# The prompt's keys are turned, and its final states taken, one place later, behind the first half of the first gate tile

## The chip, the cores and the metric

The program runs on one core of a Trainium2 chip. The metric is the device time of one execution in microseconds; the kernel before takes 1621.96 us as the median of three runs (1619.52 to 1623.79).

## What is computed

One step of a two-layer diffusion backbone on 512 latent tokens and 128 prompt tokens, width 1024. Layer 0 mixes tokens by pooling, layer 1 by bidirectional retention with 4 heads; a squared-ReLU MLP follows each. The retention of one head, cut to what matters here:

```
q, k, v, g = split(h @ w_in)                      # per head: q, k 256 wide, v, g 512 wide
q, k (latent only) are rotated by grid position
state_dir = sum over prompt tokens  zeta_dir * k^T v        # final prompt states, an output
o = intra(q, k, v) + q @ cached_state (latent only), both directions
out = (silu(g) * groupnorm(o)) @ w_out
returns y_prompt, y_sample, new_state_ret         # new_state_ret: 2 directions x 4 heads x 256 x 512
```

The final prompt states (`new_state_ret`) are read by nothing else in the kernel: they are computed and written out.

## The kernel before

All products are done in a split form: each fp32 operand is cut into a high part (a copy on ScalarE, ACT, line 144) and a low part (a subtraction on VectorE, DVE, line 145), and `mm3` (lines 205 to 207) issues three matmuls: high by high, high by low, low by high. A `gemm` is one output tile of 128 features by 320 tokens (half of the 640): 8 blocks of the contraction times 3 matmuls, 24 in all.

Layer 1 runs a loop over the four heads (`for hd in range(HEADS)`). Ahead of each pass lie the values of the head (`values`, lines 990 to 992 for the products) and its queries and keys (`take`, lines 935 to 948: a copy of two halves, the prompt's part `pr` by line 938, the rotation). For head 0 the order is keys, then values; for heads 1 to 3 it is values, output projection of the head before, queries and keys, and the very last thing ahead of the pass is the second key tile. Then one pass is, in the order of the program:

1. `states`, first part: two transposes of the prompt's keys into one PSUM tile (line 1005), and for each direction a scaled high part on ACT (line 1011) and a low part on DVE (line 1012), called kz below.
2. `attention`, ahead of its products: decay tables xi and dm (lines 1045 to 1050; dm is an Exp on ACT), and the first operands from the cached state: a load of 256 KB on SP's queue (line 1055), its mean (lines 967, 968), its centred high and low part (lines 974, 975), and a decayed query (line 1058).
3. `step1`: one step of the layer's modulation vectors: it turns the sums of the last step (four transposes, line 394, a reduction, line 395) and makes 16 sums on DVE (lines 387, 389).
4. gate tile 0, as two gemms of 24 matmuls, each ended by a Silu on ACT (line 1031). After each half the generator `final` is advanced by one place.
5. (head 0 alone: another `step1`), gate tile 1 in the same way, another `step1`.
6. `attend`: products with the cached state (tiles 0 and 1 of the forward direction), scores of four key tiles, outputs, then the backward direction; its later state operands are loaded and prepared as they are needed.

The second and third place of `states` are the products of one direction each: two PSUM tiles of three matmuls of 512 columns, each copied out by ACT (line 1020) and written to memory by a transfer from GpSimd's queue (line 1021). With one place taken ahead of the gate, the products of the forward direction stand behind the first half of gate tile 0 and those of the backward direction behind its second half.

The program is written in Tile: the instructions are put down in one order, and a planner makes of it, at compile time, a fixed order for each engine and gives out the slots of the pools. The working tiles of this stage (`t5`, `th`) share one pool of 7 slots of 128 by 512; the scaled prompt keys, the high and low part of the prompt's values, the decay pieces, the cached states as loaded, the decayed queries, the score tiles and the states on their way out all take their slots there. PSUM has 8 banks, all in one pool.

Of the kernel before, what the change touches and what calls it, by code (L numbers as in the profile page):

```python
# [110 lines left out]
def hybrid_kernel(ctx: ExitStack, tc: tile.TileContext, x_prompt, x_sample, state_ret, c, c_ctx, w_ada, b_ada,  # L111
# [71 lines left out]
    def weights(src, pools=(wsp,), other=0):  # L183


        k = src.shape[0] // 128
        wide = 1024 // k
        raw, parts = {}, {}

        def get(j):  # L190
            i = j * 128 // wide
            if i not in parts:
                if i // 2 not in raw:
                    raw[i // 2] = load(src[:, i // 2 * 2 * wide:(i // 2 + 1) * 2 * wide], (k, 2 * wide))
                parts[i] = split_w(raw[i // 2][:, :, i % 2 * wide:(i % 2 + 1) * wide], sub=G if i < other else V,
                                   pool=pools[i % len(pools)])
            o = j * 128 % wide
            return [z[:, :, o:o + 128] for z in parts[i]]

        return get  # L200
# [296 lines left out]
    def add_to_x(d, h, ps, gate):  # L497
        for j, cols in PARTS[h]:
            x = xT[d][:, HALVES[h]][:, cols]
            V.scalar_tensor_tensor(x, ps[:, cols], gate[:, d, j:j + 1], x, ALU.mult, ALU.add)  # L500
# [406 lines left out]
    with tc.tile_pool(name="ret", bufs=1) as rp:  # L907
# [70 lines left out]
        def values(hd):  # L978

            out = [bank() for _ in range(5)]  # L980
            c0 = 2048 + hd * DV
            for e in range(2):
                st = load(ret_w_in[0, e * 512:(e + 1) * 512, c0:c0 + 512], (4, 512))
                for f in range(2):
                    w = split_w(st[:, 2 * f:2 * f + 2])
                    for i in range(5):
                        for k in range(2):
                            hh = [z[:, i * 128:i * 128 + 128] for z in h1t[e * 4 + f * 2 + k]]
                            first, last = e == 0 and f == 0 and k == 0, e == 1 and f == 1 and k == 1
                            T.matmul(out[i], hh[0], w[0][:, k, :], start=first, stop=False)  # L990
                            T.matmul(out[i], hh[1], w[0][:, k, :], start=False, stop=False)  # L991
                            T.matmul(out[i], hh[0], w[1][:, k, :], start=False, stop=last)  # L992
            vs = [centre(out[i], *[rp.tile([128, DV], F32R, tag=f"v{i}{e}", name=nm("v")) for e in "hl"])
                  for i in range(4)]
            vpr = t5()
            vpc = rp.tile([128, DV], F32, tag="vpc", name=nm("vpc"))
            S.copy(vpr, out[4])
            V.tensor_scalar(vpc, vpr, mean_of(vpr), None, ALU.add)
            return vs, split(vpr, t5().bitcast(F32R), t5().bitcast(F32R)), vpc

        def states(hd, prm, vpr):

            pk = bank()
            for t in range(2):
                T.transpose(pk[:, t * 128:(t + 1) * 128], prm["k", t], ident)
            kz = []
            for rr in range(2):
                both = t5().bitcast(F32R)
                hi, lo = both[:, 0:256], both[:, 256:512]
                z = zeta[:, 4 * rr + hd:4 * rr + hd + 1]  # L1010
                S.activation(hi, pk[:, 0:256], AF.Copy, scale=z)
                V.scalar_tensor_tensor(lo, pk[:, 0:256], z, hi.bitcast(F32), ALU.mult, ALU.subtract)
                kz.append((hi, lo))
            yield
            for rr in range(2):
                for t in range(2):
                    pst = bank()
                    mm3(pst, [z[:, t * 128:(t + 1) * 128] for z in kz[rr]], vpr, True, True)
                    so = t5()
                    S.copy(so, pst)  # L1020
                    nc.gpsimd.dma_start(out=new_state[0, 0, rr, hd, t * 128:(t + 1) * 128, :], in_=so)
                yield

        def gates(hd):

            get = weights(ret_w_in[0, :, 4096 + hd * DV:4096 + (hd + 1) * DV])

            def one(e, mid=None, between=None):
                sg = rp.tile([128, TOK], F32, tag=f"sg{e}", name=nm("sg"))
                for h in range(2):  # L1030
                    S.activation(sg[:, HALVES[h]], gemm([get(e)], h1t, h, mid if h == 0 else None)[0], AF.Silu)
                    if between:
                        next(between, None)
                return sg
            return one

        def attention(hd, rot, prm, vs, vpc):

            lf, lb, nlb = lg[:, hd:hd + 1], lg[:, 4 + hd:5 + hd], nlg[:, 4 + hd:5 + hd]
            xi = [rp.tile([128, TOK], F32, tag=f"sg{3 - r}", name=nm("xi"))[:, 0:LAT] for r in range(2)]  # L1040
            for r in range(2):
                S.activation(xi[r], ipos[:, r, :], AF.Exp, scale=(lf, lb)[r])

            dm = rp.tile([128, 896], F32, tag="dm", name=nm("dm"))
            V.tensor_scalar(dm, npos, 0.0, lf, ALU.max, ALU.mult)
            for cols in (slice(0, 448), slice(448, 896)):
                t = t5()[:, 0:448]
                V.tensor_scalar(t, npos[:, cols], 0.0, nlb, ALU.min, ALU.mult)
                V.tensor_tensor(dm[:, cols], dm[:, cols], t, ALU.add)
            S.activation(dm, dm, AF.Exp)  # L1050

            def state_operands(r, t):

                st = t5()
                nc.sync.dma_start(out=st, in_=state_ret[0, 0, r, hd, t * 128:(t + 1) * 128, :])
                sh_, sl_ = centre(st, r5(), r5())
                qx = t5()
                V.tensor_tensor(qx, rot["q", t][0], xi[r], ALU.mult)
                return sh_, sl_, split(qx, r5(), r5())

            first = state_operands(0, 0)
            return lambda: attend(hd, rot, prm, vs, vpc, dm, state_operands, first)
# [49 lines left out]
        def gated(hd, gate, sg, osl, po):  # L1112

            sqs = [Squares(ones_v, GN_EPS * DV / 128), Squares(ones_v, GN_EPS * DV / 128)]
            pe = [po[:, e * 128:(e + 1) * 128] for e in range(4)]
            for e in range(4):
                sqs[0].add(osl[e][:, 0:HALF])
                sqs[1].add(osl[e][:, HALF:LAT], pe[e])
            r = []
            sg.append(gate(2, lambda: r.extend([sq.rstd() for sq in sqs])))  # L1120
            us = [slots(2 * e, TOK) for e in range(4)]
            for e in range(4):
                if e == 2:
                    sg.append(gate(3))
                w = vec[:, O_GN + hd * 4 + e:O_GN + hd * 4 + e + 1]
                V.scalar_tensor_tensor(sg[e][:, 0:LAT], osl[e], w, sg[e][:, 0:LAT], ALU.mult, ALU.mult)
                V.scalar_tensor_tensor(sg[e][:, LAT:TOK], pe[e], w, sg[e][:, LAT:TOK], ALU.mult, ALU.mult)
                for h in range(2):
                    u = th()
                    V.tensor_tensor(u, sg[e][:, HALVES[h]], r[h], ALU.mult)  # L1130
                    split(u, *[z[:, HALVES[h]] for z in us[e]])
            return us
# [14 lines left out]
        for hd in range(HEADS):  # L1147
            gate = gates(hd)
            final = states(hd, qk[1], vv[1])
            next(final)  # L1150
            attn = attention(hd, *qk, vv[0], vv[2])
            step1()
            sg = [gate(0, between=final)]
            if hd == 0:
                step1()
            sg.append(gate(1, between=final))
            step1()
            us = gated(hd, gate, sg, *attn())
            step1()
            get = weights(ret_w_out[0, hd * DV:(hd + 1) * DV])  # L1160
            if hd < HEADS - 1:
                vv = values(hd + 1)
                step1()
                for n in range(KD):
                    for h in range(2):
                        add_to_x(n, h, gemm([get(n)], us, h)[0], mod[1][2])
                qk, _, singles = queries_keys(hd + 1)
                for u in singles:
                    u()
            else:  # L1170
                sq = tail(lambda n, h: gemm([get(n)], us, h)[0], mod[1][2], normed(norm2))
# [34 lines left out]
    final = []  # L1206
# [39 lines left out]
```

## Time and profile before

| what | value |
|---|---|
| median of three runs | 1621.96 us |
| lowest, highest | 1619.52, 1623.79 us |
| the profiled execution, its own time | 1622.77 us |
| its span | 1621.0 us |
| granted TensorE clock, mean | 0.994 of full speed |

The span is what the profiler sees between the first and the last instruction; the 1.77 us around it belong to the time as well. PE stands for TensorE, PEld for its weight loads, ACT for ScalarE, DVE for VectorE, SP for SyncE and its DMA queue. PE is busy for 98% of the span, so a microsecond of any other engine counts only if PE waits for it. The four passes of the head loop begin at about 626, 775, 920 and 1073 us of the span.

### The profile page before, as it was taken

To read this page: it belongs to the slowest core of one execution; us is meant where nothing else is said; L and a number is where in the kernel's file an instruction comes from. 1 tells how busy PE (TensorE), PEld (TensorE's weight loads), DVE (VectorE), ACT (ScalarE), POOL (GpSimd) and SP (SyncE) were. 2 spreads that over 40 slices of the span, in tenths; PEclk is the share of its full clock that TensorE was granted. 3 is DMA by queue.
4 is the path that set the end of the run, shared out by engine and by line. 5 is a ranking of instruction groups with operands and counts; after the bars stand their busy time and mean duration, and the time that the engine had idled before them with its cause. 6 is when DMAs were issued, how large, how long until landed. Compare 5 with 4: busy or idle time off the path is not lost. (4 is left out here: it accounts for less than half of the span.)

```text
span 1621.0 us, 24493 instructions
## 1 busy us (share of the span) xinstructions
PE 1582.8 (98%) x9897; PEld 1473.6 (91%) x9897; DVE 1164.0 (72%) x2254; ACT 727.0 (45%) x1338; POOL 11.7 (1%) x26
## 2 busy tenths in 40 slices
PE   6999999999999999999999999999999999999997
PEld 3459999999999988889889988998899999999997
DVE  6879996676766687886797678778967573554654
ACT  6747326336156354433442443353464371451640
POOL 0000000000000000000000000000000000000000
PEclk9999999999999999999999999999999999999999
DMA  9744333333314123323304241322032132131221
GB/s 356 252 141 146 105 105 104 104 124 111 105 53 156 45 70 128 96 79 130 128 29 156 63 146 64 118 92 91 26 105 79 34 124 78 53 104 53 95 75 66
DMA packets 137954, 169.83 MB, mean 105 GB/s; under 512 B 3512, under 2 KB 111472, under 8 KB 137840
## 3 DMA queue, kind: packets, MB, share of 16 engines
q1 hardware_dynamic: 134800, 161.28, 30.2%
q0 software_dynamic: 1312, 4.20, 0.8%
q10 hardware_dynamic: 1728, 2.78, 0.5%
q8 instruction: 78, 1.28, 0.3%
q14 instruction: 36, 0.29, 0.1%
HBM read 161.43 MB, written 6.82 MB: 104 GB/s over the span
## 5 line engine op out<-in xcount | busy, mean ns | idle before, releaser
L144 ACT CAST whi<-wst 128x1024 fp32r<-128x1024 f32 x245 | 254.4, 1049 | 422.5 <-PE ps L206 200.8
L145 DVE TENSOR_TENSOR wlo<-wst,whi 128x1024 fp32r<-128x1024 f32 x245 | 297.3, 1223 | 136.5 <-ACT whi L144 124.0
L205 PE MATMUL ps<-a,whi 128*128 128x320 f32 x896 | 277.2, 310 | 1.2 <-ACT a L144 1.2
L206 PE MATMUL ps<-a,whi 128*128 128x320 f32 x896 | 277.3, 310 | 0.1
L207 PE MATMUL ps<-a,wlo 128*128 128x320 f32 x896 | 276.2, 309 | 0.0
L500 DVE SCALAR_TENSOR_TENSOR xall<-ps,mod,xall 128x320 f32<-128x320 f32 (+2 forms) x288 | 115.7, 436 | 151.6 <-PE ps L207 150.4
L206 PEld LDWEIGHTS ps<-a,whi 128*128 128x128 f32 x896 | 168.2, 188 | 2.1 <-DVE a L145 1.7
L205 PEld LDWEIGHTS ps<-a,whi 128*128 128x128 f32 x896 | 167.9, 188 | 1.8 <-ACT a L144 1.7
L207 PEld LDWEIGHTS ps<-a,wlo 128*128 128x128 f32 x896 | 168.0, 188 | 0.0
L389 DVE SCALAR_TENSOR_TENSOR acc<-wst,c,acc 128x256 f32<-128x256 f32 x336 | 137.6, 483 | 0.0
L205 PE MATMUL ps<-tq,whi 128*128 128x320 f32 x288 | 89.0, 309 | 0.0
L206 PE MATMUL ps<-tq,whi 128*128 128x320 f32 x288 | 89.0, 309 | 0.0
L207 PE MATMUL ps<-tq,wlo 128*128 128x320 f32 x288 | 89.0, 309 | 0.0
L206 PE MATMUL ps<-A,whi 128*128 128x320 f32 x256 | 78.9, 309 | 0.0
L205 PE MATMUL ps<-A,whi 128*128 128x320 f32 x256 | 78.9, 312 | 0.0
L207 PE MATMUL ps<-A,wlo 128*128 128x320 f32 x256 | 78.2, 309 | 0.0
L145 DVE TENSOR_TENSOR a<-t,a 128x320 fp32r<-128x320 f32 x128 | 61.8, 488 | 22.7 <-ACT a L144 22.2
L435 ACT ACTIVATE t<-xall 128x320 f32<-128x320 f32 x56 | 26.0, 471 | 81.2 <-DVE xall L500 81.2
L852 ACT ACTIVATE t<-t 128x320 f32<-128x320 f32 x128 | 60.5, 473 | 1.8
L144 ACT CAST a<-t 128x320 fp32r<-128x320 f32 x128 | 58.5, 457 | 1.5
L207 PEld LDWEIGHTS ps<-tq,wlo 128*128 128x128 f32 x288 | 54.1, 188 | 0.0
L205 PEld LDWEIGHTS ps<-tq,whi 128*128 128x128 f32 x288 | 54.1, 188 | 0.0
(406 smaller groups left out, 4004.4 us busy)
## 6 DMA issues: line engine op xcount, KB each, us to landing
wst<-in_mlp_w_dram SPq DMA_DIRECT2D x64, 1024.0 KB, 5.3
wst<-in_w_ada_dram SPq DMA_DIRECT2D x46, 1024.0 KB, 6.0
wst<-in_ret_w_in_dram SPq DMA_DIRECT2D x24, 1024.0 KB, 5.2
wst<-in_ret_w_out_dram SPq DMA_DIRECT2D x8, 1024.0 KB, 5.0
t<-in_state_ret_dram SPq DMA_DIRECT2D x16, 256.0 KB, 5.5
out_dram<-t POOLq DMA_DIRECT2D x16, 256.0 KB, 2.9
xt<-in_x_sample_dram SPq DMA_DIRECT2D x4, 512.0 KB, 4.8
both<-in_w_ada_dram SPq DMA_DIRECT2D x2, 1024.0 KB, 7.3
```

Of the source, the lines that this page charges most:

```text
L144: S.copy(hi, src)
L145: sub.tensor_tensor(lo, src, hi.bitcast(F32), ALU.subtract)
L205: T.matmul(out, wh, ah, start=first, stop=False, skip_group_check=more)
L206: T.matmul(out, wh, al, start=False, stop=False, skip_group_check=more)
L207: T.matmul(out, wl, ah, start=False, stop=last, skip_group_check=more)
L389: V.scalar_tensor_tensor(acc[j], w[:, k], by, acc[j], ALU.mult, ALU.add)
L435: S.activation(sq[:, o:o + t.shape[-1]], t, AF.Square)
L500: V.scalar_tensor_tensor(x, ps[:, cols], gate[:, d, j:j + 1], x, ALU.mult, ALU.add)
L852: S.activation(f, r, AF.Square)
```

## The change

The first advance of `final` ahead of the pass is left out. Everything that `states` does happens one place later: the two transposes and the scaled keys behind the first half of gate tile 0, the forward direction's products behind its second half, the backward direction's behind the first half of gate tile 1, and the call behind the second half of gate tile 1 finds the generator at its end. No instruction is added or taken away.

```
         for hd in range(HEADS):
             gate = gates(hd)
             final = states(hd, qk[1], vv[1])
-            next(final)
             attn = attention(hd, *qk, vv[0], vv[2])
             step1()
             sg = [gate(0, between=final)]
```

`final` is used by the loop of `one` in `gates` (`if between: next(between, None)` behind each half), which is unchanged.

## Rows read from the trace of the kernel before

**Rows 1.** The page's head and its part 1 (busy us, share of the span, instructions) for TensorE and its weight loads.

```profile
span 1621.0 us, 24493 instructions
...
PE 1582.8 (98%) x9897; PEld 1473.6 (91%) x9897; DVE 1164.0 (72%) x2254; ACT 727.0 (45%) x1338; POOL 11.7 (1%) x26
```

**Rows 2.** Busy time of each engine in a stretch: the whole retention part, 585 to 1180 us (columns: the stretch, its length, busy us and instructions of PE, PEld, DVE, ACT and POOL, granted clock, DMA share, GB/s).

```profile
...
585.00:1180.00 595.00, 586.03 (x3374) 533.98 (x3373) 465.81 (x995) 237.93 (x437) 8.71 (x16) 0.99 0.29 96
```

**Rows 3.** What PE's matmuls waited for, two stretches, 585 to 1180 us first and then heads 1 to 3 (668 to 1100 us) alone: us in total, times, longest us.

```profile
...
PE ps L1005 <- ACT pr L938: 2.8, 5, 1.4
PE ps L205 <- ACT r L144: 2.3, 5, 0.8
...
PE ps L1005 <- ACT pr L938: 0.8, 3, 0.2
```

**Rows 4.** PE in order of time where head 0's values begin (start us, busy us, engine, line, operation, idle before and what ended it), and below it the clock of the stretch behind the gap (TensorE alone).

```profile
...
595.66 0.39 PE L991 MATMUL ps<-whi,h0l 128*128 128x512 f32 x1
597.41 0.33 PE L1005 MATMUL ps<-tab_sb,pr 128*128 128x128 f32 x1 [1.35 <-ACT pr L938]
598.16 0.66 PE L394 MATMUL ps<-tab_sb,acc 128*128 128x128 f32 x4 [0.42 <-DVE t L946]
599.55 0.47 PE L1005 MATMUL ps<-tab_sb,pr 128*128 128x128 f32 x1 [0.73 <-ACT pr L938]
599.68 0.78 PE L992 MATMUL ps<-wlo,h0h 128*128 128x512 f32 x1
...
600.00:603.00 3.00, 3.00 (x9) 0.50 0.00 0
```

**Rows 5.** DVE in order of time in the same stretch.

```profile
...
598.28 1.22 DVE L145 TENSOR_TENSOR wlo<-wst,whi 128x1024 fp32r<-128x1024 f32 x1
```

**Rows 6.** PE in order of time through the pass of head 1.

```profile
...
775.58 0.39 PE L205 MATMUL ps<-h0h,whi 128*128 128x320 f32 x1
...
776.37 0.33 PE L1005 MATMUL ps<-tab_sb,pr 128*128 128x128 f32 x1 [0.25 <-ACT pr L938]
...
779.76 0.39 PE L205 MATMUL ps<-t,t 128*128 128x512 f32 x1
...
781.15 0.30 PE L205 MATMUL ps<-h0h,whi 128*128 128x320 f32 x1
...
784.67 0.39 PE L205 MATMUL ps<-t,t 128*128 128x512 f32 x1
...
793.44 0.47 PE L205 MATMUL ps<-r,r 128*128 128x512 f32 x1
...
796.29 0.39 PE L205 MATMUL ps<-A,A 128*128 128x512 f32 x1
...
797.09 1.21 PE L205 MATMUL ps<-r,r 128*128 128x512 f32 x4
...
801.13 0.39 PE L206 MATMUL ps<-r,r 128*128 128x512 f32 x1
```

**Rows 7.** DVE in order of time through the same pass.

```profile
...
777.48 0.48 DVE L1012 SCALAR_TENSOR_TENSOR t<-ps,zeta,t 128x256 fp32r<-128x256 f32 x1
...
786.67 2.07 DVE L389 SCALAR_TENSOR_TENSOR acc<-wst,c,acc 128x256 f32<-128x256 f32 x5
788.65 0.69 DVE L1058 TENSOR_TENSOR t<-q,xi 128x512 f32<-128x512 f32 x1
789.26 0.68 DVE L967 TENSOR_REDUCE cm<-t 128x1 f32<-128x512 f32 x1
...
790.92 0.75 DVE L975 SCALAR_TENSOR_TENSOR r<-t,cm,r 128x512 fp32r<-128x512 f32 x1 [0.79 <-ACT r L974]
...
794.63 5.63 DVE L389 SCALAR_TENSOR_TENSOR acc<-wst,c,acc 128x256 f32<-128x256 f32 x14
```

**Rows 8.** ACT in order of time through the same pass.

```profile
...
776.73 0.48 ACT L1011 ACTIVATE t<-ps,zeta 128x256 fp32r<-128x256 f32 x1 [0.42 <-PE ps L1005]
...
782.01 1.28 ACT L1050 ACT_TABLE_LOAD   x1
...
787.51 1.07 ACT L1020 COPY t<-ps 128x512 f32<-128x512 f32 x2
```

**Rows 9.** SP's queue in order of time in the same pass, and, below it, the loads of the cached states over all heads from issue to landing.

```profile
...
778.52 8.07 SPq L1055 DMA_DIRECT2D t<-in_state_ret_dram  x2
...
DMA to landing us min/median/max: 3.5/5.5/6.6
```

**Rows 10.** Head 0, where its sums end and the products with the cached states begin: DVE, then ACT, then PE, each in order of time.

```profile
...
644.44 0.69 DVE L967 TENSOR_REDUCE cm<-t 128x1 f32<-128x512 f32 x1
...
646.31 5.62 DVE L389 SCALAR_TENSOR_TENSOR acc<-wst,c,acc 128x256 f32<-128x256 f32 x14
651.86 0.14 DVE L968 TENSOR_SCALAR cm<-cm 128x1 f32<-128x1 f32 x1
...
653.25 0.72 ACT L974 ACTIVATE r<-t,cm 128x512 fp32r<-128x512 f32 x1
...
647.53 0.39 PE L205 MATMUL ps<-A,A 128*128 128x512 f32 x1
...
653.25 0.71 PE L1102 MATMUL ps<-pr,pr 128*128 128x128 f32 x4
654.53 1.21 PE L205 MATMUL ps<-r,r 128*128 128x512 f32 x4 [0.56 <-ACT r L144]
```

More of the change, by code (lines that the diff above doesn't have):

```diff
@@ L1149, in hybrid_kernel @@
             final = states(hd, qk[1], vv[1])
-            next(final)
             attn = attention(hd, *qk, vv[0], vv[2])
```

## The prediction

> **What bounds the kernel now.** I read the page's first part, then the stretch that holds the head loop, then what PE waited for, and only then each engine in order of time through single passes. The reader is to see that PE is the bound and has almost nothing left to give back here: 98% busy over the span [rows 1], and 586.03 of 595 us in the retention part [rows 2]. So 9 us is all the idle time that any change of order in this part could remove. PE waits 2.8 us of it for the prompt's part of a key tile at line 1005, which is exactly the instruction that this change moves; a similar 2.3 us goes to operands of the cached states [rows 3]. DVE and ACT matter only where a matmul stands behind them.
>
> **The waits at the transposes, heads 1 to 3.** The second key tile is the last thing ahead of a pass, and the transposes come right behind it. ACT has two copies and a scaling to do on the last 128 columns, so the second transpose waits 0.25 us, with the gate's matmuls queued behind it on PE [rows 6]; the three heads together wait 0.8 us [rows 3]. Behind the first half of the gate tile the key part has been ready for over 3 us (24 matmuls take 784.67 - 781.15 = 3.52 us [rows 6]), so this wait goes. What is next on PE is the gate's own matmuls, whose weights were cut long before. Gain: 3 x 0.25 = 0.75 us.
>
> **The same, head 0.** Here keys come ahead of values, and the planner had put both transposes into a hole of PE: 1.35 and 0.73 us of waiting at 597 to 599.5 us [rows 4]. It looks like the larger half of the 2.8 us, but the hole has another owner. The next matmul, at 599.68, needs the low part of the first value weights, which DVE makes from 598.28 for 1.22 us, until 599.50 [rows 5]. Without the transposes PE waits for that instead. I cost this at 0; the bounds are 0 (the low part is late anyway) and a gain of 0.2 us (599.68 - 599.50). TensorE runs at the lower of its two levels (granted 0.50) behind the hole [rows 4]; the hole stays, so that stays. If the two transposes land later among gate matmuls they cost their own time there: from 775.58, two matmuls of 0.15 us, then the transpose, then the next matmul at most 0.1 us behind it. That is 0.2 us for the head, which I set against the 0.2 above.
>
> **The moved products and their cover.** Scaled keys now start after the first half of the gate tile instead of before it. In head 1 they ran on ACT at 776.73 and on DVE from 777.48 [rows 7, 8]. After the change the transposes come at about 779.5 and ACT can scale at about 780, between a Silu and the decay's Exp (its table switch is at 782.01 [rows 8]). On DVE they then stand behind the 16 modulation sums, which precede them in the program. That DVE does take work in this way is seen at the sums' end: the query of line 1058 begins at 788.65, the instant that they stop [rows 7]; and in head 0 a mean of 0.14 us waits from 645.1 until 651.86 behind the sums [rows 10]. So the low parts would be ready not at 778 but when the sums end, 788.65 less the 2 x 0.48 us that have left the queue ahead of them, 787.7, plus 0.48: about 788.2. PE has other work until then: the second half of gate tile 0 (to about 783.1), the high parts of the first products (4 x 0.23 us, to 784.0) and the first half of gate tile 1 (3.52 us, to 787.5), then the high parts of the backward direction (0.9 us, to 788.4). If the planner lays PE's order out like that, the cover is just enough, and the cost is nothing; without that cover it is the second rival.
>
> **What is behind them.** The four states on their way out take pool slots and leave through GpSimd's queue, which has nothing else to do. The next load of a cached state takes its slot after them. SP issues it in head 1 at about 786.2 (the pair ends at 778.52 + 8.07 = 786.59 [rows 9]); it then has its mean taken at 789.26, in the pause of DVE ahead of the next sums, and is needed on PE at 797.09 [rows 6, 7]. With the last product done one gate half later, or only when the low parts arrive, the issue moves by 3.5 to 4.5 us to about 790. Landing takes 3.5 to 6.6 us [rows 9], so the state comes at 793.5 to 796.6, when the next sums have begun, and the mean may fall behind them, to 800.2: the pattern of head 0 before. Then PE must live on what needs no state: 12 matmuls on the first state (793.44 to 796.29 [rows 6]), then 24 for four score tiles (0.23 us each, 5.5 us, as head 0 does them from 647.53 to 653.0 [rows 10]), to 801.8. Mean 0.69, its scaling 0.15 and the centred copy 0.72 give 801.8 as well. The end is a stall between 0 and 0.84 us in a head: head 0 before shows both the 0.28 us ahead of its small product at 653.25 and the 0.56 us behind it [rows 10]. I take 0.2 us, nearer to zero, since the cover and the operand meet; 0.6 us for heads 1 to 3. A gain is excluded, because PE has no wait at this place now.
>
> In head 0 the reduction at 644.44 was done ahead of the sums; now its state lands behind 644, and 0.69 us of reduction moves in front of the 651.86 mean, with the centred copy and PE's 654.53 behind it [rows 10]. Bounds: 0 (ACT was busy until 653.25 anyway) and 0.69. I take 0.6, since the wait at 654.53 is real and the query behind it moves too.
>
> **Sum.** -0.75 (waits of heads 1 to 3) + 0 (head 0's transposes) + 0.6 (cached state, heads 1 to 3) + 0.6 (head 0) = about +0.5 us. Bounds: -0.95 (all gains, no cost) and -0.75 + 3 x 0.84 + 0.69 + 0.2 = +2.7. Against the profiled execution's 1622.77 us that is 1623.3; it lies 0.8 us above the median of the runs, so against 1621.96 I say 1622.5.
>
> **Rivals.**
> First, nothing of it reaches PE: the planner pulls work forward as it finds room, as it did with head 0's transposes [rows 4], and mean and state keep their place. Then only the 0.75 us is gained: 1621.2. For it: fixed order by readiness in the rows. Against: the slots are handed on only when the states are out.
> Second, slower: matmuls run in their queue's order, so if the low-high product of the forward direction is put straight behind its two companions, at about 783.6, PE stands until the low part of 788.2, with gate tile 1 queued behind it. That is 4.5 us in each of heads 1 to 3 (in head 0 DVE has no sums there), some 13 us: 1635. It decides from the point at which the planner expects the low part earlier than DVE really has it. For it: the plan is fixed before the run, and sums of 5 to 7 us stand ahead. Against: in the present trace a planned order rarely costs PE more than 0.5 us. The Trainium skill, "TensorE: Matmul & The Clock Gate", "Part 2: What happens when you issue a matmul", speaks against the change in the same way: matmuls stay in program order and only weight loads are pulled ahead. The trace agrees: the gate's matmul stands at 776.45 behind the 0.25 us wait of a transpose that it doesn't need.
> Third, milder: the states come late and only three score tiles find PSUM banks. PE then lacks 6 x 0.23 = 1.4 us of cover in heads 1 to 3, besides the terms above: 1622.5 + 4.2 = 1626.7.
> Fourth, faster: the order of head 0 shifts so that the hole of 4 us closes, with the half-rate stretch behind it (about 3 us, half of it lost): up to 5.4 + 0.75 = 6 us, 1616. Against it: the low part at 599.50 stands on a DVE that is busy without a break.
>
> **How the numbers follow.** Forecast 60%, first rival 14%, second 10%, third 11%, fourth 5%. 0.3% (4.9 us) is about what a measurement of this kernel can tell from no change. Forecast and first rival are within it, and most of the third; the second and some of the third are slower, the fourth is faster: faster 5%, same 80%, slower 15%. The range runs from 1618.5 (best sum, less what three runs scatter, about 2 us) to 1627.5 (the third rival with a little scatter), and leaves out the second and the fourth, 15%.
>
> **What would show it.** Right: no wait at line 1005; its transposes at about 779.5 in head 1; the low parts of line 1012 behind the sums; the second load of line 1055 some 4 us later; PE's idle time in 585 to 1180 us still 8 to 12 us; the hole at 596 to 599.7 still there. Wrong: a wait of 2 us or more at line 207 for the low part of the scaled keys (second rival), idle time ahead of the second cached state above 1 us in several heads (third), a value product that starts well before 599.5 (fourth).

## The result and the profile after

The changed kernel takes 1632.8 us (median of six runs, 1631.62 to 1633.55) where the kernel before took 1622.24 us in six runs of its own on the same chip (1619.52 to 1623.79): a ratio of 1.0063, interval 1.0053 to 1.0074. It is slower by 10.6 us. The forecast was 1622.5 us with a range to 1627.5.

Page of the changed kernel, head and part 1, against [rows 1]: PE is still the bound, but the span has grown by 10.8 us with the same 9897 matmuls and the same counts on the other engines (the 19 instructions more in the head are none of these).

```profile
span 1631.8 us, 24512 instructions
...
PE 1589.7 (97%) x9897; PEld 1480.3 (91%) x9897; DVE 1163.3 (71%) x2254; ACT 726.2 (45%) x1338; POOL 11.6 (1%) x26
```

Stretches of the changed kernel (columns as in [rows 2]): the whole retention part, heads 1 to 3 between the markers explained below, six microseconds of head 1, and three stretches in heads 1, 2 and 3. In the whole retention part PE is busy 5.4 us less than in [rows 2] in the same length and idle for 14.4 us, where the prediction had 8 to 12, so the first thing to ask is what it waits for. The DMA share of 0.97 in the third line and the granted clocks of the last three are needed further down.

```profile
...
585.00:1180.00 595.00, 580.59 (x3335) 529.15 (x3333) 455.77 (x979) 235.86 (x433) 8.68 (x16) 0.99 0.29 94
677.00:1133.90 456.90, 447.49 (x2591) 410.05 (x2591) 339.55 (x727) 170.94 (x309) 6.45 (x12) 0.99 0.30 97
789.00:795.00 6.00, 6.00 (x39) 5.62 (x38) 0.91 (x2) 3.68 (x6) 1.79 (x4) 1.00 0.97 352
805.00:809.00 4.00, 4.00 (x12) 2.92 (x11) 3.78 (x7) 0.11 (x1) 0.00 (x0) 0.57 1.03 357
956.00:960.00 4.00, 4.00 (x17) 2.99 (x18) 4.00 (x7) 1.35 (x4) 0.00 (x0) 1.00 0.91 293
1109.00:1113.00 4.00, 4.00 (x12) 2.90 (x11) 3.52 (x6) 0.13 (x1) 0.00 (x0) 0.57 0.96 371
```

What PE waited for, 585 to 1180 us (us in total, times, longest), against [rows 3]:

```profile
...
PE ps L1102 <- DVE t L1083: 6.7, 3, 2.9
PE ps L992 <- DVE wlo L145: 3.0, 1, 3.0
PE ps L205 <- ACT t L1011: 2.1, 4, 0.7
PE ps L207 <- DVE t L1012: 0.7, 3, 0.2
```

The wait at line 1005 is gone, as the change meant. At the top stands one that the kernel before doesn't have at all: line 1102, the small product that makes the prompt's own scores, is released by DVE's line 1083, which multiplies a score tile of the latent tokens with its decay: 6.7 us, once in each of heads 1 to 3. Two smaller ones are the moved keys themselves: line 1011 (2.1 us, of which 0.16 us is head 0's) and line 1012 (0.7 us). The 3.0 us at line 992 are the old hole of head 0 under its real owner's name.

To see in which heads the loss arises, one marker is enough: the first matmul of line 465 with `ones_v`, the variance at the end of each pass. First its row in the kernel before, then in the changed one (lowest, median and longest ns; first and last start in us):

```profile
...
L465 PE MATMUL ps<-sqacc,ones_v x16: 432/432/537, 678.2 to 1124.7; 128*128 128x320 f32 x16
```

```profile
...
L465 PE MATMUL ps<-sqacc,ones_v x16: 432/432/538, 677.0 to 1133.9; 128*128 128x320 f32 x16
```

The first start is at the end of head 0, the last is in head 3. At the first one the changed kernel is 1.2 us ahead (678.2 to 677.0; 0.3 us of it arise before head 0's values). From there to head 3 the kernel before takes 446.5 us and the changed one 456.9: heads 1 to 3 lose 10.4 us. The same stretch of the kernel before, to set beside the second line of the changed kernel's stretches:

```profile
...
678.20:1124.70 446.50, 443.97 (x2590) 407.31 (x2589) 341.27 (x728) 171.26 (x309) 6.47 (x12) 1.00 0.30 101
```

PE stands idle for 9.4 us of it instead of 2.5, and is busy 3.5 us longer. Behind the last marker the remaining 1.6 us are lost.

PE of the changed kernel in order of time: head 0's first product with the low part of the value weights, the pass of head 1, and the same small product in head 3.

```profile
...
599.23 0.50 PE L992 MATMUL ps<-wlo,h0h 128*128 128x512 f32 x1 [3.05 <-DVE wlo L145]
...
774.57 0.39 PE L205 MATMUL ps<-h0h,whi 128*128 128x320 f32 x1
...
778.16 0.38 PE L1005 MATMUL ps<-tab_sb,pr 128*128 128x128 f32 x2
...
782.73 0.50 PE L205 MATMUL ps<-t,t 128*128 128x512 f32 x1 [0.66 <-ACT t L1011]
...
787.23 0.73 PE L207 MATMUL ps<-t,t 128*128 128x512 f32 x2 [0.24 <-DVE t L1012]
...
789.39 0.39 PE L207 MATMUL ps<-t,t 128*128 128x512 f32 x1
...
801.53 0.39 PE L207 MATMUL ps<-A,A 128*128 128x512 f32 x1
803.98 0.71 PE L1102 MATMUL ps<-pr,pr 128*128 128x128 f32 x4 [2.06 <-DVE t L1083]
...
1107.71 0.71 PE L1102 MATMUL ps<-pr,pr 128*128 128x128 f32 x4 [2.94 <-DVE t L1083]
```

In head 1 the last of the 24 matmuls of the scores starts at 801.53, and then PE stands until 803.98. What the small product lacks is not its operands (`pr`, copied by ACT long before) but, by the program, a PSUM bank: four of the eight hold the outputs and four the score tiles that DVE has not yet masked. The trace names only the instruction that releases it. Behind that wait the granted clock is low in heads 1 and 3 (0.57 in 805 to 809 us and in 1109 to 1113 us, so for most of them at the lower of the two levels), which costs 4 x 0.43 = 1.7 us each time; head 2 keeps 1.00. Now DVE, the engine that PE waits for, in order of time, with the same mean in heads 2 and 3 below:

```profile
...
784.71 2.06 DVE L389 SCALAR_TENSOR_TENSOR acc<-wst,c,acc 128x256 f32<-128x256 f32 x5
786.70 0.48 DVE L1012 SCALAR_TENSOR_TENSOR t<-ps,zeta,t 128x256 fp32r<-128x256 f32 x1
787.78 0.48 DVE L1012 SCALAR_TENSOR_TENSOR t<-ps,zeta,t 128x256 fp32r<-128x256 f32 x1 [0.60 <-ACT t L1011]
...
794.78 0.69 DVE L967 TENSOR_REDUCE cm<-t 128x1 f32<-128x512 f32 x1 [4.27 <-DMA t<-in_state_ret_dram]
795.38 1.21 DVE L145 TENSOR_TENSOR wlo<-wst,whi 128x1024 fp32r<-128x1024 f32 x1
...
797.64 5.62 DVE L389 SCALAR_TENSOR_TENSOR acc<-wst,c,acc 128x256 f32<-128x256 f32 x14
803.18 0.14 DVE L968 TENSOR_SCALAR cm<-cm 128x1 f32<-128x1 f32 x1
803.24 1.27 DVE L1083 TENSOR_TENSOR t<-ps,dm 128x512 f32<-128x512 f32 x2
...
946.80 0.69 DVE L967 TENSOR_REDUCE cm<-t 128x1 f32<-128x512 f32 x1 [3.98 <-DMA t<-in_state_ret_dram]
...
1098.51 0.69 DVE L967 TENSOR_REDUCE cm<-t 128x1 f32<-128x512 f32 x1 [5.15 <-DMA t<-in_state_ret_dram]
```

This is the reading that matters. The reduction for the mean of the second cached state (line 967) stands on DVE ahead of the next sums (x14 at 797.64). Its operand is still being loaded, so DVE stands idle for 4.27, 3.98 and 5.15 us, and everything queued behind it starts late. The sums begin at 797.64, and behind them come the scaling of that mean (line 968, 803.18) and the masks of the scores (803.24). In [rows 7] the same sums begin at 794.63, 3.0 us earlier, in a pass that begins 1.0 us later (775.58 in [rows 6], 774.57 here): relative to the pass they are 4.0 us late, 23.07 us behind the first gate matmul instead of 19.05.

Two things that PE needs end with these late sums: the bank that a masked score tile gives free, and the second cached state itself, whose centred high part ACT can make only behind the scaling (803.36 to 804.08); the products with it begin at 804.64. Had the bank been free, by these rows PE would have stood for the state instead, to about 804.1. And not all of the 4.0 us is the load's. In three kernels further down (the early load, the mean on ACT, the mean behind the sums) DVE no longer stands for that load, and their sums begin 20.68 us behind the first gate matmul. So about 2.4 us belong to the load. The other 1.6 us remain in all three: PE reaches the transposes of the step (line 394), which its sums wait for, 1.05 us later in the pass (793.13 - 774.57 against 793.09 - 775.58), and DVE makes the low part of the next weights (line 145, 795.38) ahead of the sums instead of behind them.

Why the load lands so late: SP's queue in order of time, what SP's queue waited for from 765 to 812 us (us, times, longest), and GpSimd's writes of the final states, all in head 1.

```profile
...
789.58 0.34 SPq L1055 DMA_DIRECT2D t<-in_state_ret_dram  x1
```

```profile
...
SPq L1055 <- PE ps L207: 2.6, 1, 2.6
```

```profile
...
788.64 1.07 POOL L1021 DMA_DIRECT2D out_dram<-t  x2 [146.72 <-ACT t L1020]
790.06 1.18 POOL L1021 DMA_DIRECT2D out_dram<-t  x2 [0.35 <-ACT t L1020]
```

The load is issued at 789.58, 15.0 us after the first gate matmul (774.57); in [rows 9] it was 778.52 + 8.07 - 0.34 = 786.25, 10.7 us after the 775.58 of [rows 6]. SP waits for PE's line 207 there: the slot comes free when the last moved product (789.39) has read its operands. It then takes 5.2 us to land (794.78 - 789.58), in a stretch in which the DMA engines are 0.97 busy with the four writes, the gate's weights and this load.

ACT of the changed kernel in the same pass: why the scaled keys are late in the first place, and, in the last line, the centred high part of the second state.

```profile
...
778.90 1.28 ACT L1050 ACT_TABLE_LOAD   x1
780.19 0.95 ACT L1050 ACTIVATE dm<-dm 128x896 f32<-128x896 f32 x1
781.59 0.72 ACT L974 ACTIVATE r<-t,cm 128x512 fp32r<-128x512 f32 x1 [0.45 <-DVE cm L968]
782.22 0.45 ACT L1011 ACTIVATE t<-ps,zeta 128x256 fp32r<-128x256 f32 x1
...
803.36 0.72 ACT L974 ACTIVATE r<-t,cm 128x512 fp32r<-128x512 f32 x1 [9.09 <-DVE cm L968]
```

The transposes were issued at 778.16, and ACT could have scaled at about 779. But the Exp's table load, the Exp and the centring of the first cached state are ahead of it in ACT's order, so the scaled key comes at 782.22 and PE waits 0.66 us for it.

### The profile page after: what moved, and what is told of

Read it like the earlier page. It is cut to its first block, busy times and chain, and to the rows that moved or that the text cites. A ratio compares the mean times of both kernels' runs of the same rounds, so it can differ in the third digit from the quotient of the medians.

```text
span 1631.8 us, 24512 instructions
## 1 busy us (share of the span) xinstructions
PE 1589.7 (97%) x9897; PEld 1480.3 (91%) x9897; DVE 1163.3 (71%) x2254; ACT 726.2 (45%) x1338; POOL 11.6 (1%) x26
## 4 chain that ended last, share of the span: by engine, by line
PE 82%; DVE 8%; DMA 5%; ACT 4%; issue 1%; ACTq 0%; DVEq 0%
PE ps L206 23%; PE ps L205 23%; PE ps L207 23%; PE ps L283 2%; DVE acc L389 2%; PE ps L992 2%; DMA wst<-in_mlp_w_dram 2%; PE ps L991 2%; PE ps L990 2%; ACT whi L144 1%; DMA wst<-in_w_ada_dram 1%; DVE wlo L145 1%; DMA t<-in_state_ret_dram 1%; PE ps L630 1%; PE ps L465 1%
## 5 line engine op out<-in xcount | busy, mean ns | idle before, releaser
L206 PEld LDWEIGHTS ps<-tq,whi 128*128 128x128 f32 x288 | 54.1, 188 | 0.0
L205 PEld LDWEIGHTS ps<-tq,whi 128*128 128x128 f32 x288 | 54.1, 188 | 0.0
```

The lines of the kernel that those rows point to most:

```text
L205: T.matmul(out, wh, ah, start=first, stop=False, skip_group_check=more)
L206: T.matmul(out, wh, al, start=False, stop=False, skip_group_check=more)
```

## The experiments

Times are ratios to the kernel before on the same chip, with their intervals.

**Both halves of the change apart.** The change moves two things: the scaled keys (transposes, lines 1011 and 1012) and the products with them. First, keys at their old place, products one place later (on the kernel before):

```diff
                 kz.append((hi, lo))
             yield
+            yield
```

> Half of the change alone: the prompt's keys are turned and scaled ahead of the pass as before, and only the state products come one place later. Theory A (the products hand their pool slots on late, so the second cached state of each head is loaded late, its mean holds up DVE's sums, and PE runs out of other work ahead of line 1102): the wait at line 1102 stays in heads 1 to 3, 1.5 to 3 us each, and the waits on the scaled keys (lines 1011 and 1012, 0.9 us a head in the changed kernel) go: 1628 to 1631 us. Theory B (the low part of the scaled keys stands behind the sums, and that alone holds up everything): as the kernel before, 1621 to 1623 us.

Measured: 1621.25 us, 0.9988 (0.9977 to 0.9999), in theory B's range and not in theory A's: no wait at line 1102 is left. The late products alone cost nothing. DVE and PE in head 1:

```profile
...
793.48 5.62 DVE L389 SCALAR_TENSOR_TENSOR acc<-wst,c,acc 128x256 f32<-128x256 f32 x14
799.02 0.68 DVE L967 TENSOR_REDUCE cm<-t 128x1 f32<-128x512 f32 x1
```

```profile
...
801.67 1.20 PE L205 MATMUL ps<-r,r 128*128 128x512 f32 x4 [0.49 <-ACT r L144]
```

Here too the second load is issued late, at 788.38 (13.95 us after the first gate matmul at 774.43). But the mean falls behind the sums, which begin at 793.48, as early in the pass as in the kernel before (19.05 us), and PE waits 0.49 us for the centred state. This is the pattern that the prediction had for the changed kernel. So theory A was right that the load comes late, and wrong that a late load must stall the pass. A second measurement of this kernel, to see whether it beats the kernel before:

> Keys turned ahead of the pass, products one place later, in more rounds: if its lead is real, 1620 to 1622 us and an interval of the ratio below 1; if not, an interval across 1.

Measured: 1620.73 us, 0.9991 (0.9982 to 1.0000). At or a little under the kernel before, not clearly faster.

The other half: keys late, products at their old places (the changed kernel without the `yield` behind the keys):

```diff
                 kz.append((hi, lo))
-            yield
```

> The other half alone: the keys are turned and scaled behind the first half of gate tile 0, but the products keep their places of before (forward behind the first half, backward behind the second half). Theory A: the low part is still made at the end of the sums, so the last product ends within 1 us of where it ends in the changed kernel, and the wait at line 1102 stays: 1627 to 1632 us. Theory B: the same or a little less, 1629 to 1632. A third theory, that only the place of the products counts: 1621 to 1624.

Measured: 1647.37 us, 1.0153 (1.0134 to 1.0172). Now the products stand right behind their keys and PE waits for each, 16.2 us at line 1011 in all:

```profile
...
787.23 0.79 PE L205 MATMUL ps<-t,t 128*128 128x512 f32 x1 [4.17 <-ACT t L1011]
```

All three theories missed this time. The keys come no earlier than in the changed kernel, and without the distance between them and their products PE stands for 4.17 us instead of 0.66. So the expensive half is the late keys: directly here, and in the changed kernel through what follows the products.

**The load.** If the load's late slot is the cause, issuing it early must take the wait away with keys and products left late (on the changed kernel):

```diff
-            def state_operands(r, t):
-
+            def state_load(r, t):
                 st = t5()
                 nc.sync.dma_start(out=st, in_=state_ret...)
+                return st
+
+            def state_operands(r, t):
+                st = held.pop() if held and (r, t) == (0, 1) else state_load(r, t)
...
+            held = []
             first = state_operands(0, 0)
+            held.append(state_load(0, 1))
```

> The changed kernel, with one edit: the load of the second cached state (forward, tile 1) is asked for right behind the first one, ahead of the states in the order of the slots. Theory A: the load lands before the sums of the third step, the wait at line 1102 and the half-rate stretch behind it go, and what stays is the 0.9 us a head on the scaled keys: 1622 to 1626 us. Theory B: nothing changes, 1631 to 1634 us.

Measured: 1624.81 us, 1.0013 (1.0003 to 1.0024), in theory A's range: some 8 us come back (0.63% has become 0.13%). SP, DVE and PE's waits:

```profile
...
775.16 3.37 SPq L1054 DMA_DIRECT2D t<-in_state_ret_dram  x2
```

```profile
...
787.93 0.66 DVE L967 TENSOR_REDUCE cm<-t 128x1 f32<-128x512 f32 x1
...
796.08 5.63 DVE L389 SCALAR_TENSOR_TENSOR acc<-wst,c,acc 128x256 f32<-128x256 f32 x14
```

```profile
...
PE ps L205 <- ACT t L1011: 2.1, 4, 0.7
...
PE ps L207 <- DVE t L1012: 0.7, 3, 0.2
```

Both loads leave SP within 3.4 us, the mean is taken at 787.93 between the two scaled keys, ahead of the sums without holding them up, and the wait at line 1102 is gone with the low clock behind it. The keys' own waits are unchanged, 2.1 and 0.7 us. They are not all that is left: PE also waits 1.0 us for centred states and once, in head 3, 1.95 us for a low part (line 206). The profiled execution is one of the slower ones (1627.01 us); its heads 1 to 3 take 451.4 us from marker to marker, so 5.5 of the 10.4 us come back there. The early load added to the kernel with early keys tells whether it is worth something by itself:

> Keys turned ahead of the pass as before, products one place later, and the second cached state's load asked for right behind the first. If the waits on cached states that are left (some 1.5 us in all) come from that load: they go, 1619 to 1621 us. If they come from the order behind DVE's sums: as without the early load, 1620.5 to 1622 us.

Measured: 1623.09 us, 1.0007 (0.9998 to 1.0017), above both ranges. It isn't; it only takes away what the change caused.

**The writes beside the load.** The changed kernel without the writes of the final states of heads 1 to 3:

```diff
-                    nc.gpsimd.dma_start(out=new_state[...], in_=so)
+                    if hd == 0: nc.gpsimd.dma_start(out=new_state[...], in_=so)
```

> The changed kernel without the writes of the final states of heads 1 to 3 (they are computed and copied, but only head 0's go out, so the third output is incomplete). If the load of the second cached state lands late because the four writes of a head now leave together with it and with the gate weights: DVE's wait on it falls from 4 to 5 us to under 2.5 us, and the wait at line 1102 under 1 us a head: 1622 to 1627 us. If only its late issue counts: DVE still waits over 3.5 us, 1630 to 1633 us.

Measured: 1626.25 us, 1.0027 (1.0016 to 1.0039). SP, DVE, and a stretch of head 1 (columns as in [rows 2]):

```profile
...
790.83 0.34 SPq L1055 DMA_DIRECT2D t<-in_state_ret_dram  x1
```

```profile
...
795.05 0.69 DVE L967 TENSOR_REDUCE cm<-t 128x1 f32<-128x512 f32 x1 [3.04 <-DMA t<-in_state_ret_dram]
```

```profile
...
790.00:796.00 6.00, 6.00 (x40) 5.69 (x38) 2.13 (x4) 4.38 (x8) 0.00 (x0) 1.00 0.66 218
```

The first gate matmul of this pass begins at 777.02, so the load is issued after 13.8 us instead of 15.0: without the writes a tile on its way out gives up its slot sooner, and SP waits for ACT's copy (line 1020) and no more for the last product. And it lands in 4.2 us instead of 5.2, with a DMA share of 0.66 instead of 0.97 (4.2 against 4.9 in head 2, 5.6 against 6.1 in head 3). Together the state is some 2 us earlier, DVE stands 3.04 us instead of 4.27 (in heads 2 and 3 2.99 and 4.37 instead of 3.98 and 5.15; the time is in the first expectation's range, but its "under 2.5" is not reached), and only one wait at line 1102 is left (1.2 us, head 3): the cover reaches nearly that far, and the last two microseconds of lateness are what PE sees. The run changes issue and landing at once, so it doesn't divide the loss between them. The Trainium skill, "DMA: Bandwidth & Descriptors", "Issuing engines are not separate DMA queues", says that transfers issued from SP, ACT and GpSimd run on the same 16 DMA engines and interleave there. The two landings fit that.

**The order on DVE.** The rival to the late load is the mean's place ahead of the sums. Three kernels take the mean out of the way. First the mean on ACT:

```diff
-                sh_, sl_ = centre(st, r5(), r5())
+                if (r, t) == (0, 1):
+                    m = rp.tile([128, 1], F32, tag="cm", ...)
+                    sh_, sl_ = r5(), r5()
+                    S.activation(sl_, st, AF.Copy, scale=-1.0 / DV, accum_out=m)
+                    S.activation(sh_, st, AF.Identity, bias=m)
+                    V.scalar_tensor_tensor(sl_, st, m, sh_.bitcast(F32), ALU.add, ALU.subtract)
+                else:
+                    sh_, sl_ = centre(st, r5(), r5())
```

> The changed kernel, with the mean of the second cached state of each head (forward, tile 1) taken on ACT by the sum that an activation can write beside its output, in place of the reduction on DVE. Theory A', as it stands after the first four runs (the planner puts that reduction ahead of DVE's next sums, DVE stands 4 to 5 us on the state's load, and so the sums, the masking of the scores and PE behind them come late): DVE's wait on the load goes, the sums begin by 794 us in head 1 (797.1 in the changed kernel), the wait at line 1102 falls under 0.5 us a head and the half-rate stretch goes: 1622 to 1626 us. Rival (the late load itself leaves PE without work): the wait moves to PE's products with that state, 2 to 3 us a head: 1629 to 1632 us.

> The kernel with that mean on ACT once more, in more rounds, since its first four times lay between 1627.4 and 1633.4. If its waits decide: 1626 to 1629 us. If the clock behind the hole of head 0 decides (granted clock 0.991 to 0.996 in the first runs): again spread over 6 us, with the time going with the clock.

Measured: 1631.24 us, 1.0059 (1.0041 to 1.0077), and measured again 1629.02 us, 1.0041 (1.0029 to 1.0054). The wait at line 1102 is gone and the sums begin at 795.95 (2.4 us earlier relative to the pass, whose first gate matmul is at 775.27; not by 794 as theory A' had it). PE waits 2.5 us for centred states (line 205 on ACT's `r`; 3.1 us in the second), where the changed kernel has none of this and the kernel before 2.3 us [rows 3]. The time is in the rival's range, but the 2 to 3 us a head that the rival expected there are not. Single runs scatter over 6 us both times, and not with the clock (the slowest of the second series, 1632.47 us, has 0.994, its median run 0.992), so neither expectation of the second one holds, and the scatter stays unexplained. By the ratios 0.6 to 3.6 us come back, less than with the early load. The same edit on the kernel with early keys:

> The same, with the mean of the second cached state on ACT. If the 1.5 us of waits on cached states that are left come from its mean standing behind DVE's sums: they go, 1619 to 1621 us; if not, 1620.5 to 1622.5 us.

Measured: 1624.69 us, 1.0010 (1.0002 to 1.0019), above both ranges: no gain.

Second, the mean forced behind the sums by a copy of one column of their accumulator into its target (`accs` holds the accumulators of the step):

```diff
+                    V.tensor_copy(m, accs[1][:, 0:1])
+                    V.tensor_reduce(m, st, axis=AX.X, op=ALU.add)
```

> The changed kernel, with the mean of the second cached state of each head held behind DVE's sums of the step before it (a copy of one column of the last sum into the mean's tile, 0.1 to 0.2 us, makes the order). Theory A' (the mean planned ahead of the sums makes DVE stand on a load that lands late): sums begin by 794.5 us in head 1, no DVE wait on that load, the wait at line 1102 falls under 0.7 us a head although load and states are as late as in the changed kernel: 1623 to 1627 us. Rival (the late load itself): PE waits 2 us or more a head for that state: 1630 to 1634 us.

Measured: 1633.58 us, 1.0074 (1.0061 to 1.0087), not better than the changed kernel. DVE and PE in head 1:

```profile
...
794.39 5.62 DVE L389 SCALAR_TENSOR_TENSOR acc<-wst,c,acc 128x256 f32<-128x256 f32 x14
```

```profile
...
803.38 0.94 PE L1116 MATMUL ps<-scp,vpc 128*128 128x128 f32 x6 [1.90 <-DVE scp L1113]
```

The sums begin 3.2 us earlier than in the changed kernel, and 2.4 us earlier relative to the pass (its first moved product begins at 781.87, against 782.73). That is what theory A' expected of DVE, and the time is in the rival's range all the same, but not by the rival's wait for the state. The planner now laid another small product of the prompt (line 1116) ahead of the rest, and PE waits as long for the masked scores of the prompt that it needs (line 1113, made at 803.04 behind the sums): 7.0 us in four heads. The wait has moved by a few lines. So the mean's place alone is not the whole cause.

Third, the sums of the second step behind the whole attention:

```diff
+            products = attn()
             step1()
-            us = gated(hd, gate, sg, *attn())
+            us = gated(hd, gate, sg, *products)
```

> The changed kernel, with one edit: the modulation step that stands behind gate tile 1 is put behind the products of attend, so that the mean of the second cached state no longer competes with its sums. Theory A: the load stays late (issue at about 789.5 in head 1), but the mean is done at landing, so the wait at line 1102 goes: 1622 to 1627 us. Theory B: nothing changes at the scaled keys, which stand behind the earlier sums: 1630 to 1634 us.

Measured: 1691.23 us, 1.0424 (1.0405 to 1.0442). It tells nothing of the mean, since the sums themselves become what PE waits for:

```profile
...
PE ps L394 <- DVE acc L389: 22.7, 3, 7.6
```

**A place in between.** The keys not behind the gate half but behind the attention's first operands, ahead of the sums of `step1`; the products then stay at their old places (on the changed kernel):

```diff
             attn = attention(hd, *qk, vv[0], vv[2])
+            next(final)
             step1()
```

> The first advance is made behind the prelude of attention and ahead of the modulation step, so the keys are turned before the gate tile but planned behind the decay's work. Theory A': low parts are not behind the sums, the products are not late, the second load keeps its time: no wait at lines 1102, 1011 or 1012: 1620 to 1623 us. A theory that the place behind the decay's Exp on ACT is what costs: PE waits about 0.7 us at line 1011 and some at 1102, 1625 to 1630 us.

Measured: 1625.75 us, 1.0032 (1.0021 to 1.0044). The marker of line 465 and the one large wait:

```profile
...
L465 PE MATMUL ps<-sqacc,ones_v x16: 432/433/537, 681.3 to 1127.4; 128*128 128x320 f32 x16
```

```profile
...
PE ps L205 <- ACT t L1011: 3.9, 1, 3.9
```

From head 0 to head 3 it takes 1127.4 - 681.3 = 446.1 us, as the kernel before does, and none of its waits at lines 1011, 1012 or 1102 falls in heads 1 to 3. Its loss, 3.1 us at the first marker (681.3 against 678.2), lies in head 0, where PE waits 3.9 us for the scaled key, which ACT makes at 632.84, behind the Exp's table load, the Exp and the centring of the first state. So the time is in the second theory's range, and its mechanism is there in head 0 alone. So in heads 1 to 3 the keys may stand behind the attention's operands at no cost, as long as they are ahead of the sums. The costly step is the one past the sums and the first gate half.

## Why the prediction was wrong

**The step that failed** is the one headed "What is behind them". It had the chain up to the arrival: "the issue moves by 3.5 to 4.5 us" (4.3 us relative to the pass), "the state comes at 793.5 to 796.6" (794.78, or 795.8 with the pass's 1.0 us). Then: "the mean may fall behind them, to 800.2: the pattern of head 0 before", and from that "a stall between 0 and 0.84 us in a head". It let the mean slide and left the sums in their place. But DVE's order is fixed before the run. In the changed kernel the reduction stayed ahead of the sums, as in [rows 7], and DVE waits with the sums behind it; only its scaling lies behind them, as in head 0 before (651.86 in [rows 10]). Here the late operand did not slide behind the work that follows; it held that work up. The stall was 2.2 us a head (6.7 / 3) instead of 0.2, before 3.4 us for the low clock, which the sum did not have. The pattern that I described does occur, with 0.49 us of waiting, in the kernel with early keys, where the planner had laid the mean behind the sums and the sums are on time. The row of 789.26 in [rows 7] was read as "the pause of DVE"; it was a position in a queue.

**The third rival** had the outcome's direction and half of its mechanism (states late), but its cover was not at fault: all 24 score matmuls were there, as the forecast said. A PSUM bank did run short, but one step later, for the small product, because DVE's masks came late. Its sign, more than 1 us of idle time ahead of the second state in several heads, did appear. Its 1626.7 us was 6 us too low.

**The moved keys' cover** was right in kind and off in size. The low parts did come behind the sums (786.70 and 787.78; forecast 787.7 for the first, 786.7 with the pass's shift), and the product that needs them waits 0.24 us, so the second rival did not come true. The high part was put at "about 780" on ACT and came at 782.22, behind the Exp and the centring of the first state: 0.66 us a head at line 1011, which with the 0.24 us at line 1012 the sum had put at nothing.

**The gains** of heads 1 to 3 were right. The wait at line 1005 went (0.8 us in heads 1 to 3); the transposes came at 778.16 (forecast 779.5, less 1.0); the hole of head 0 stayed, its product starting at 599.23 behind 3.05 us of waiting for the weights' low part. The 0.6 us that head 0 was to lose did not come: the mean of its second state is done at 643.04, ahead of the sums, and the wait at 654.53 [rows 10] is gone, so at the first marker the kernel is 1.2 us ahead.

**The account of heads 1 to 3**, marker to marker: PE's waits there are 6.7 (line 1102) + 2.0 (line 1011) + 0.7 (line 1012) = 9.4 us after, and 1.6 (line 205 on ACT's `r`) + 0.8 (line 1005) + 0.2 (line 206 on DVE's `r`) = 2.6 us before. That is 6.8 us more, and 3.4 us for the low clock (805 to 809 and 1109 to 1113 us) make 10.2 of the 10.4 us; PE's busy time says the same, 3.5 us more.

**Shown and open.** That the late load, with its reader planned ahead of the sums, holds up the pass is shown: with keys and products as late, the early load gives some 8 us back. (The planner makes a new order for every kernel, so each of these runs moves a little more than its edit.) That late products alone cost nothing is shown, and so is that keys ahead of the sums cost nothing in heads 1 to 3. How the loss divides between the late issue and the slower landing stays open, since the run without writes changed both and PE sees only what exceeds the cover. Open is why the planner lays the mean behind the sums in one kernel and ahead of them in the other: its estimates are in no trace. Since the kernel with the mean behind the sums only got another wait, the cause is the late load together with the order planned around it, not that order alone. The 1.6 us behind the last marker are no wait: PE is idle for 9.8 us there instead of 12.8, but its 3269 matmuls keep it busy for 488.08 us instead of 483.51, at a lower granted clock in two places (0.94 instead of 0.97 in the 55.3 us behind the marker, 0.97 instead of 0.98 in the last 120 us or so). Whether the change brings that or it is this one execution is open.

No version tried clearly beats the kernel before. The nearest is early keys with late products, at 0.9988 and 0.9991, which is within 0.3%.

## What to carry to other kernels

When a step is moved, follow the pool slots that it frees to the load that takes them next, and then ask where that load's first reader stands in its engine's fixed order: everything queued behind the reader waits with it. A pause in which an engine does a short instruction is a position, not a free choice; only where a trace shows that instruction behind the long work may the late case be priced that way. When a move takes a producer and its consumer along, measure each move by itself, since here one half cost nothing and the other 24 us.

## What the runs showed of the hardware

A load of 256 KB took 4.2 us from its issue to its reader with the DMA engines 0.66 busy, and 5.2 us with them 0.97 busy, in the same place of the pass. The runs of the two differ also in when the load was issued.

Waits of PE of like length did not always bring the low clock. In the changed kernel the granted clock fell to 0.57 over 4 us behind the waits of 2.06 and 2.94 us (heads 1 and 3) and stayed at 1.00 behind that of 1.74 us (head 2). But in other kernels it fell behind shorter waits (1.79 us in head 3 of the second run with the mean on ACT, 1.87 us in head 2 of the kernel with the mean behind the sums) and stayed at 1.00 behind 1.90 and 1.99 us in heads 1 and 3 of the latter and 1.95 us in head 3 of the kernel with the early load. A wait of about 2 us may cost 1.7 us more, or nothing; its length alone doesn't tell which.
